# Where three feed-forward blocks split their gates into high and low halves: a change in the order around the first group of seven products

## The chip, the cores and the metric

The kernel runs on one core of one Trainium2 chip. The metric is the device time of one execution in microseconds (us); lower is better. The core has a matrix engine (PE, with its weight loads listed apart as PEld), a vector engine (DVE), a scalar engine (ACT), a general engine (POOL), and a queue (SP) from which nearly all DMA transfers are issued. Each engine works through its own row of instructions strictly in the order of the program; a semaphore holds an instruction until what it needs is there.

## The reference

Two layers of a streaming encoder on 256 positions of width 1024, all in float32. Each layer is a feed-forward block, a mixer (a convolution module in layer 0, latent attention in layer 1) and a second feed-forward block. There are thus four feed-forward blocks, and the change touches the second, third and fourth.

```python
def swiglu_ffn(h, w1, w3, w2):
    return (jax.nn.silu(h @ w1) * (h @ w3)) @ w2
...
for i in range(DEPTH):
    h = h + FFN_RES_WEIGHT * swiglu_ffn(rmsnorm(h, ffn_norm1[i]), ffn1_w1[i], ffn1_w3[i], ffn1_w2[i])
    m = rmsnorm(h, mix_norm[i])
    ...
    h = h + FFN_RES_WEIGHT * swiglu_ffn(rmsnorm(h, ffn_norm2[i]), ffn2_w1[i], ffn2_w3[i], ffn2_w2[i])
return rmsnorm(h, final_norm)
```

D_MODEL is 1024, D_FF is 2816.

## The kernel before

**Products in three parts.** Matrix products run on operands split into a high half (rounded) and a low half (the rest). `mm3` makes one product of three matrix instructions: row halves high times weight low (L332 in the profile, shown as `lo,X..`), high times high (L335) and row low times weight high (L336).

**Weight blocks.** A weight block is 128 x 2048 float32 (1 MB). SP fetches it to one of four `raw` buffers. ACT writes its high half `hi` in two casts of 128x1024, and DVE writes its low half `lo = raw - hi` in two subtractions of 128x1024 (ordinary blocks: L246 and L247; blocks of a group of seven: L214 and L200). `hi` and `lo` have five buffers each.

**Chunks.** A feed-forward block goes through its 2816 hidden columns in six chunks, `c` = 0 to 5. An ordinary chunk uses four weight blocks, two of `w1` and two of `w3`. After a chunk, for each of the two row blocks (`tb`), ACT applies silu (L956), DVE multiplies the two branches (L958, or L258 where it is marked urgent) and transposes 32x32 squares (L478), and five DMAs turn the gate through DRAM memory (L482 and L487). Then ACT casts the turned gate to its high half `Gh` and DVE writes its low half `Gl` (both L853). These casts and low splits are kept in the list `gates`, two pairs for each chunk; nothing on PE needs them before the down product `@ w2`, which starts after chunk 5.

**The group of seven.** In the second, third and fourth block, chunk 3 is a 2x2 product of submatrices done with seven products instead of eight (`seven_products`). Its weights are made by `load_seven`: four fetched blocks and four differences on DVE (128x2048, L200 `raw<-raw,raw`). The third of these differences, in `load_seven` at `j == 2`, is the one that makes the weight of the third product. PE adds the products into four banks c11, c21, c12 and c22, and three sums connect them: ACT copies c11 to c21 after the first product and c22 to `kept` after the second (both L258), DVE adds c21 and `kept` into c12 after the third product and into c22 after the fifth (both L258, `u<-u,p`). The order of the products is: c11, c22, c21, c11, c21, c12, c21. The same function also serves the first products of `@ w2`; there `late` is given and the lines of the change do nothing.

**What sets the order.** The program is written with a scheduler that orders each engine's row by its own timeline; `urgent` gives an operation priority, and `order(a, b)` adds the rule that a stands behind b on its engine. The change is in such rules.

Of the kernel before, what the change touches and what calls it, by code (L numbers as in the profile page):

```python
# [22 lines left out]
NT = S // P  # L23
# [19 lines left out]
PIECES = 2  # L43
# [46 lines left out]
def trunk(ctx: ExitStack, tc: tile.TileContext, x, xt, first, pos, invf, gfin, wdw,  # L90
          f1w13, f1w2, f2w13, f2w2, cw1, cw2, wa, wuq, wukv, wo, wpair, out):
    nc = tc.nc
# [12 lines left out]
    def uid(s):  # L105
        n_uid[0] += 1
        return f"{s}_{n_uid[0]}"
# [46 lines left out]
    def order(ins, first):  # L154
        tc.add_manual_dep(ins.ins, first.name, mybir.DependencyInfo(
            mybir.DependencyClass.NoSync, mybir.DependencyReason.DATA), reason="order")

    def behind(ins):

        for first in ahead_of.get(ins.ins.engine, [])[-BEHIND:]:  # L160
            order(ins, first)


    casts = {}

    turns = []
    last_read = [None]
# [14 lines left out]
    def fetched(src):  # L182
        raw = rawp.tile([P, HB], F32, tag="raw", name=uid("raw"))
        dma = nc.sync.dma_start(raw, src)
        if turns:
            order(dma, turns[-1].ins)
        return raw

    def load_seven(j, four, b, pieces):
        hi = wp.tile([P, HB], F32R, tag="hi", name=uid("hi"))  # L190
        lo = wp.tile([P, HB], F32R, tag="lo", name=uid("lo"))
        n = len(loaded)
        if j == 0:
            b[11], b[12] = fetched(four[0]), fetched(four[1])
        elif j == 1:
            b[22] = fetched(four[3])
        elif j == 2:
            b[21] = fetched(four[2])
        def sub(out, left, right):
            ins = nc.vector.tensor_sub(out, left, right)  # L200
            behind(ins)
            return ins

        if j == 1:
            sub(b[11], b[12], b[11])
            sub(b[12], b[22], b[12])
        elif j == 2:
            sub(b[11], b[22], b[11])
        elif j == 6:
            sub(b[11], b[21], b[11])  # L210
        raw = b[(11, 11, 11, 21, 12, 22, 11)[j]]
        for i in range(pieces):
            c = slice(i * HB // pieces, (i + 1) * HB // pieces)
            casts[n, i] = nc.scalar.copy(hi[:, c], raw[:, c]), sub(lo[:, c], raw[:, c], hi[:, c].bitcast(F32))  # L214
            behind(casts[n, i][0])
        return hi, lo

    def load(src, pieces=1):
        if isinstance(src, tuple) and src[0] == "seven":
            return load_seven(*src[1:], pieces)  # L220
# [31 lines left out]
    def urgent(f):  # L252

        def g(*args, **kw):
            traced = nc.cur_bb.bb.instructions
            n = len(traced)
            with tc.high_priority():
                r = f(*args, **kw)  # L258
            last = {ins.engine: ins for ins in traced[n:]}
            for engine, ins in last.items():  # L260
                ahead_of.setdefault(engine, []).append(ins)
            return r
        return g

    def load_ahead(ahead=W_BUFS - 2):
        load_to(min(len(blocks), n_used[0] + ahead))
# [5 lines left out]
    def weights(n=1, more=True):  # L272
        out = []
        for _ in range(n):
            n_used[0] += 1
            if more:
                load_ahead()
            else:
                load_ahead(0)
            out.append(loaded[n_used[0] - 1])  # L280
        return out
# [48 lines left out]
    def mm3(o, ah, al, bh, bl, start, stop, after=(), seeded=False):  # L330

        mm = nc.tensor.matmul(o, ah, bl, start=start, stop=False, skip_group_check=seeded)  # L332
        for a in after:
            order(mm, a.ins)
        nc.tensor.matmul(o, ah, bh, start=False, stop=False, skip_group_check=seeded)  # L335
        return nc.tensor.matmul(o, al, bh, start=False, stop=stop, skip_group_check=seeded)  # L336
# [31 lines left out]
    def seven_products(xh, xl, forms, banks, late={}):  # L368


        def rows(a, tb):
            k = slice(4 * a, 4 * a + 4)
            return xh[:, k, tbs(tb)], xl[:, k, tbs(tb)]

        def product(a, b, fresh):
            load_ahead(W_BUFS - 1)
            (hi, lo), = weights(1, False)
            for k in range(4):
                c = slice(k * 512, k * 512 + 512)
                before[:] = [mm3(b, a[0][:, k], a[1][:, k], hi[:, c], lo[:, c], fresh and k == 0, k == 3, before, True)]  # L380

        n0 = n_used[0]
        before = []
        c11, c21, c12, c22 = banks[0, 0], banks[1, 0], banks[0, 1], banks[1, 1]
        product(rows(0, 0), c11, True)
        first = urgent(nc.scalar.copy)(c21, c11)
        for cast in late.values():
            order(cast, first.ins)
        product(forms[0], c22, True)
        kept = tmp.tile([P, 512], F32, tag="s", name=uid("p5"))  # L390
        last = urgent(nc.scalar.copy)(kept, c22)
        product(forms[1], c21, False)
        add = urgent(nc.vector.tensor_add)(c12, c21, kept)
        order(casts[n0 + 5, 0][1], add.ins)
        for high, low in gates[-NT:] if not late else ():
            order(high, last.ins)
            order(low, add.ins)
        low_gates = [low for high, low in gates[-NT:] if not late]
        product(rows(1, 0), c11, False)
        product(forms[2], c21, False)  # L400
        add = urgent(nc.vector.tensor_add)(c22, c21, kept)
        order(casts[n0 + 6, 0][1], add.ins)
        for low in low_gates[1:]:
            order(low, casts[n0 + 6, PIECES - 1][1].ins)
        product(forms[3], c12, False)
        product(rows(1, 1), c21, False)
# [8 lines left out]
    def tbs(tb):  # L415
        return slice(tb * P, (tb + 1) * P)
# [336 lines left out]
    class Rows:  # L753
# [6 lines left out]
        def seven(self, forms, late):  # L760
            seven_products(self.zh, self.zl, forms, self.o, late)
# [72 lines left out]
    gates = []  # L834
# [7 lines left out]
    def ffn_in(act, X, make_next, beside, apart, seven_up, seven_down):  # L842
# [41 lines left out]
        for c in range(6):  # L884
# [9 lines left out]
            if c in seven_up:  # L894
                for key in ((0, 0), (0, 1), (1, 1), (1, 0)):
                    u[key] = bank("A", "u")
                seven_products(X.xh, X.xl, forms, {(tb, m): b for (m, tb), b in u.items()})
                beside()
                beside()
# [788 lines left out]
    class Rows512:  # L1688

        n = {"ht": 0, "hb": 0}  # L1690
# [109 lines left out]
def build(shapes):  # L1800
    import concourse.bacc as _bacc

    nc = _bacc.Bacc("TRN2", target_bir_lowering=False, num_devices=1, dynamic_dma_scratch_size=1024)
    args = [nc.dram_tensor(f"in_{n}", s, mybir.dt.from_np(np.dtype(d)), kind="ExternalInput").ap()
            for n, s, d in shapes]
    out = nc.dram_tensor("out", (S, D), F32, kind="ExternalOutput").ap()
    with tile.TileContext(nc, schedule_with_timeline_sim=True) as tc:
        trunk(tc, *args, out)
    return nc
# [9 lines left out]
```

## Time and profile before

| what | value |
|---|---|
| time before, median of 3 runs | 897.49 us (896.9 to 898.99) |
| the profiled execution's own time | 896.07 us |
| its span, first to last instruction | 894.3 us |
| PE busy | 886.9 us (99%) |
| DVE busy | 743.1 us (83%) |
| ACT busy | 571.8 us (64%) |
| mean granted clock of PE | 0.999 |

Rows of the timeline start with the time from the span's start and the busy time, both in us; then come engine, line of the kernel before, operation, what is written from what, shapes, and how many instructions are put together (x2). In brackets stands how long the engine sat idle just before, and what ended that. Buffer numbers are left out there.

### The profile page before, as it was taken

The numbers are of one execution on the slowest core, as the hardware profiler recorded it, in microseconds if no ns is written. First come the engines' busy times: TensorE is split into PE (matmuls) and PEld (weight loads), VectorE is DVE, ScalarE is ACT, GpSimd is POOL, SyncE is SP. The second block draws the span as 40 slices with busy tenths as digits, with TensorE's granted clock in tenths as the row PEclk, the third lists the DMA queues.
The fourth block names the chain that finished last, engine by engine and source line by source line (L and its number), as shares of the span: only waits on it lengthen the run. The fifth ranks groups of instructions, "written<-read, shape, count | busy, mean of one in ns | idle before, by whom it ended". The sixth has DMA issues, their size and how long they took to land.

```text
span 894.3 us, 12241 instructions
## 1 busy us (share of the span) xinstructions
PE 886.9 (99%) x4221; PEld 745.9 (83%) x4221; DVE 743.1 (83%) x1083; ACT 571.8 (64%) x993; POOL 104.2 (12%) x227
## 2 busy tenths in 40 slices
PE   9999999999999999999999999999999999999997
PEld 7888888898988888888888888888899888888886
DVE  6787789579998999999588989995768579989973
ACT  7966458488886646667375566673677566474752
POOL 1000000069962000000010000001400010000000
PEclk9999999999999999999999999999999999999999
DMA  9987629834215864939759369495635349378541
GB/s 330 375 303 274 232 59 355 295 121 172 106 60 194 289 258 144 374 109 388 259 175 339 118 218 357 123 392 182 223 142 189 141 154 342 104 260 317 180 196 48
DMA packets 71055, 198.94 MB, mean 222 GB/s; under 512 B 12369, under 2 KB 41937, under 8 KB 51665
## 3 DMA queue, kind: packets, MB, share of 16 engines
q1 hardware_dynamic: 70560, 197.47, 61.8%
q8 instruction: 33, 0.54, 0.2%
q10 hardware_dynamic: 432, 0.69, 0.2%
q14 instruction: 30, 0.24, 0.1%
HBM read 181.87 MB, written 16.25 MB: 222 GB/s over the span
## 4 chain that ended last, share of the span: by engine, by line
PE 92%; DVE 4%; ACT 2%; DMA 1%; issue 0%; SPq 0%; POOL 0%; DVEq 0%; ACTq 0%
PE u L336 16%; PE u L335 16%; PE u L332 16%; PE o L335 9%; PE o L336 9%; PE o L332 9%; PE gate L1005 2%; PE u L411 2%; DVE acc L1094 2%; PE u L1005 2%; PE tp L446 1%; PE a L335 1%; PE a L332 1%; PE a L336 1%; PE nope L336 1%; PE nope L332 1%
## 5 line engine op out<-in xcount | busy, mean ns | idle before, releaser
L247 DVE TENSOR_TENSOR lo<-raw,hi 128x1024 fp32r<-128x1024 f32 (+1 forms) x236 | 276.2, 1212 | 38.8 <-ACT hi L246 37.6
L246 ACT CAST hi<-raw 128x1024 fp32r<-128x1024 f32 (+1 forms) x238 | 236.8, 1044 | 89.3 <-DMA raw<-in_f2w 30.8
L332 PE MATMUL u<-lo,Xh 128*128 128x512 f32 x612 | 238.4, 389 | 0.1
L336 PE MATMUL u<-hi,Xl 128*128 128x512 f32 x612 | 238.3, 389 | 0.0
L335 PE MATMUL u<-hi,Xh 128*128 128x512 f32 x612 | 238.1, 389 | 0.0
L332 PEld LDWEIGHTS u<-lo,Xh 128*128 128x128 f32 x612 | 114.9, 188 | 24.5 <-ACT Xh L598 0.5
L336 PEld LDWEIGHTS u<-hi,Xl 128*128 128x128 f32 x612 | 114.9, 188 | 24.3 <-DVE Xl L465 0.5
L335 PEld LDWEIGHTS u<-hi,Xh 128*128 128x128 f32 x612 | 114.9, 188 | 23.8
L214 ACT CAST hi<-raw 128x1024 fp32r<-128x1024 f32 x98 | 97.7, 1050 | 51.8 <-DVE raw L200 44.9
L200 DVE TENSOR_TENSOR lo<-raw,hi 128x1024 fp32r<-128x1024 f32 x98 | 115.6, 1216 | 7.1 <-ACT hi L214 7.1
L332 PE MATMUL o<-lo,Gh 128*128 128x512 f32 (+1 forms) x276 | 106.6, 386 | 0.0
L335 PE MATMUL o<-hi,Gh 128*128 128x512 f32 (+1 forms) x276 | 106.5, 386 | 0.0
L336 PE MATMUL o<-hi,Gl 128*128 128x512 f32 (+1 forms) x276 | 106.5, 386 | 0.0
L437 POOL TENSOR_TENSOR ms<-ss 128x1 f32<-128x1 f32 x16 | 8.1, 510 | 597.6 <-ACT junk L429 597.6
L200 DVE TENSOR_TENSOR raw<-raw,raw 128x2048 f32<-128x2048 f32 x28 | 63.9, 2283 | 1.8 <-DMA raw<-in_f2w 0.9
L332 PEld LDWEIGHTS o<-lo,Gh 128*128 128x128 f32 x276 | 51.8, 188 | 10.5
L335 PEld LDWEIGHTS o<-hi,Gh 128*128 128x128 f32 x276 | 51.9, 188 | 10.5
L336 PEld LDWEIGHTS o<-hi,Gl 128*128 128x128 f32 x276 | 51.8, 188 | 10.4
L1094 DVE SCALAR_TENSOR_TENSOR acc<-V,dw,acc 128x128 f32<-128x128 f32 (+1 forms) x174 | 53.9, 391 | 0.0
L1115 ACT ACTIVATE prod<-V,dw 128x128 f32<-128x128 f32 (+1 forms) x128 | 45.6, 415 | 1.8 <-POOL Y L1116 1.0
L956 ACT ACTIVATE s<-u,R 128x512 f32<-128x512 f32 (+1 forms) x48 | 30.9, 647 | 24.8 <-PE u L336 24.1
L797 DVE SCALAR_TENSOR_TENSOR h<-o,rh,h 128x512 f32<-128x512 f32 (+1 forms) x18 | 12.9, 719 | 29.2 <-PE o L336 29.2
(265 smaller groups left out, 1257.7 us busy)
## 6 DMA issues: line engine op xcount, KB each, us to landing
raw<-in_f2w SPq DMA_DIRECT2D x66, 1024.0 KB, 6.2
raw<-in_f1w SPq DMA_DIRECT2D x62, 1024.0 KB, 6.5
raw<-in_cw SPq DMA_DIRECT2D x12, 1024.0 KB, 5.5
gd<-gt SPq DMA_DIRECT2D x160, 64.0 KB, 3.0
gb<-gd SPq DMA_DIRECT2D x24, 256.0 KB, 2.8
rows<-gd SPq DMA_DIRECT2D x16, 256.0 KB, 4.4
raw<-in_wo SPq DMA_DIRECT2D x4, 1024.0 KB, 4.9
hd<-rows SPq DMA_DIRECT2D x56, 64.0 KB, 2.4
```

Source lines behind the costliest of these rows:

```text
L200: ins = nc.vector.tensor_sub(out, left, right)
L214: casts[n, i] = nc.scalar.copy(hi[:, c], raw[:, c]), sub(lo[:, c], raw[:, c], hi[:, c].bitcast(F32))
L246: casts[len(loaded), i] = (nc.scalar.copy(hi[:, c], raw[:, c]), low.tensor_sub(lo[:, c], raw[:, c], hi[:, c].bitcast(F32)))
L247: low.tensor_sub(lo[:, c], raw[:, c], hi[:, c].bitcast(F32)))
L332: mm = nc.tensor.matmul(o, ah, bl, start=start, stop=False, skip_group_check=seeded)
L335: nc.tensor.matmul(o, ah, bh, start=False, stop=False, skip_group_check=seeded)
L336: return nc.tensor.matmul(o, al, bh, start=False, stop=stop, skip_group_check=seeded)
L411: mm = nc.tensor.matmul(o, al if kind == "x" else ah, bl if kind == "l" else bh, start=start and n == 0, stop=stop and n == len(kinds) - 1)
L956: nc.scalar.activation(s[:, :w], u[0, tb][:, :w], AF.Silu, scale=X.r[tb])
L1005: mm = nc.tensor.matmul(u[:, t], w[:, c], X.x[:, k, t], start=(k == 0), stop=(k == KT - 1))
L1094: dve_last.append(nc.vector.scalar_tensor_tensor(out if j == j1 - 1 else y, v, w, y, op0=ALU.mult, op1=ALU.add))
L1115: prods_last.append(nc.scalar.activation(p, v, AF.Copy, scale=w))
```

## The change

Two rules are replaced. For the third chunk's gates (`gates[-NT:]`, chunk 2): before, both casts stood behind the copy of c22 and both low splits behind the sum into c12, the second low split also behind the low half of the seventh block; now the first cast stands behind the sixth block's last high cast, the second behind the seventh block's last high cast, and both low splits behind the seventh block's last low half. For the second chunk's gates (`gates[-2 * NT:-NT]`, chunk 1): a new rule puts their low splits behind the third weight difference, which `load_seven` now keeps in `thirds`.

```diff
+    thirds = {}
...
         elif j == 2:
-            sub(b[11], b[22], b[11])
+            thirds[n] = sub(b[11], b[22], b[11])
...
         kept = tmp.tile([P, 512], F32, tag="s", name=uid("p5"))
-        last = urgent(nc.scalar.copy)(kept, c22)
+        urgent(nc.scalar.copy)(kept, c22)
         product(forms[1], c21, False)
         add = urgent(nc.vector.tensor_add)(c12, c21, kept)
         order(casts[n0 + 5, 0][1], add.ins)
-        for high, low in gates[-NT:] if not late else ():
-            order(high, last.ins)
-            order(low, add.ins)
-        low_gates = [low for high, low in gates[-NT:] if not late]
+        for high, low in gates[-2 * NT:-NT] if not late else ():
+            order(low, thirds[n0 + 2].ins)
+        late_gates = gates[-NT:] if not late else ()
         product(rows(1, 0), c11, False)
         product(forms[2], c21, False)
         add = urgent(nc.vector.tensor_add)(c22, c21, kept)
         order(casts[n0 + 6, 0][1], add.ins)
-        for low in low_gates[1:]:
+        for n, (high, low) in enumerate(late_gates):
+            order(high, casts[n0 + 5 + n, PIECES - 1][0].ins)
             order(low, casts[n0 + 6, PIECES - 1][1].ins)
```

PE's row is the same before and after. Below are pieces of the rows of DVE and ACT in the second feed-forward block, the first of the three; the other two blocks change in the same way. All lines of the changed kernel that stand behind the new line have a number higher by one.

On DVE around the end of the group of seven, before. `lo_3434`, `lo_3453` and `lo_3473` are the low halves of the sixth block, the seventh block and the next chunk's first block; `u_3393` is c12, `u_3392` is c22, `u_3391` is c21; `Gl_2854` is the gates' low half, from the turned gates `gb_3372` and `gb_3386` of the third chunk; `s_3532` is the group's own gate of the first row block; `raw_3235<-raw_3305,raw_3235` is the fourth weight difference:

```order
L258 TENSOR_TENSOR u_3393<-u_3391,p_553_3431 128x512
L853 TENSOR_TENSOR Gl_2854<-gb_3372,Gh_2853 128x4x128
L200 TENSOR_TENSOR lo_3434<-raw_3295,hi_3433 128x1024
L200 TENSOR_TENSOR raw_3235<-raw_3305,raw_3235 128x2048
L200 TENSOR_TENSOR lo_3434<-raw_3295,hi_3433 128x1024
L258 TENSOR_TENSOR u_3392<-u_3391,p_553_3431 128x512
L200 TENSOR_TENSOR lo_3453<-raw_3235,hi_3452 128x1024 x2
L853 TENSOR_TENSOR Gl_2854<-gb_3386,Gh_2853 128x4x128
L247 TENSOR_TENSOR lo_3473<-raw_3471,hi_3472 128x1024
L258 TENSOR_TENSOR s_3532<-s_3532,u_3393 128x512
L247 TENSOR_TENSOR lo_3473<-raw_3471,hi_3472 128x1024
```

The same place in the row of DVE after:

```order
L201 TENSOR_TENSOR lo_3434<-raw_3295,hi_3433 128x1024
L259 TENSOR_TENSOR u_3393<-u_3391,p_553_3431 128x512
L201 TENSOR_TENSOR lo_3434<-raw_3295,hi_3433 128x1024
L201 TENSOR_TENSOR raw_3235<-raw_3305,raw_3235 128x2048
L259 TENSOR_TENSOR u_3392<-u_3391,p_553_3431 128x512
L201 TENSOR_TENSOR lo_3453<-raw_3235,hi_3452 128x1024 x2
L854 TENSOR_TENSOR Gl_2854<-gb_3372,Gh_2853 128x4x128
L854 TENSOR_TENSOR Gl_2854<-gb_3386,Gh_2853 128x4x128
L259 TENSOR_TENSOR s_3532<-s_3532,u_3393 128x512
L248 TENSOR_TENSOR lo_3473<-raw_3471,hi_3472 128x1024 x2
```

The sixth block's low half moves ahead, to both sides of the first sum; both low splits of the third chunk's gates now stand behind the seventh block's low half, and with the multiplication of the gate `s_3532` they stand ahead of `lo_3473`.

On ACT at the same place, before. `hi_3433`, `hi_3452` and `hi_3472` are the high halves of the same three blocks, `Gh_2853` is the gates' high half, and `p_553_3431` is `kept`:

```order
L258 COPY p_553_3431<-u_3392 128x512
L853 CAST Gh_2853<-gb_3372 128x4x128
L214 CAST hi_3433<-raw_3295 128x1024 x2
L956 ACTIVATE s_3532<-u_3390,R_2792 128x512
L853 CAST Gh_2853<-gb_3386 128x4x128
L214 CAST hi_3452<-raw_3235 128x1024 x2
L246 CAST hi_3472<-raw_3471 128x1024 x2
```

And after:

```order
L259 COPY p_553_3431<-u_3392 128x512
L215 CAST hi_3433<-raw_3295 128x1024 x2
L854 CAST Gh_2853<-gb_3372 128x4x128
L957 ACTIVATE s_3532<-u_3390,R_2792 128x512
L215 CAST hi_3452<-raw_3235 128x1024 x2
L854 CAST Gh_2853<-gb_3386 128x4x128
L247 CAST hi_3472<-raw_3471 128x1024 x2
```

Each of the two gate casts has moved behind the weight cast that it stood ahead of.

On DVE some 20 us earlier, where the group's first weights are made, before. `lo_3294` and `lo_3304` belong to the second and third block, `raw_3235<-raw_3295,raw_3235` is the third weight difference, and `Gl_2854<-rows_139` are the low splits of earlier chunks' gates:

```order
L200 TENSOR_TENSOR lo_3294<-raw_3235,hi_3293 128x1024 x2
L853 TENSOR_TENSOR Gl_2854<-rows_139,Gh_2853 128x4x128 x2
L200 TENSOR_TENSOR raw_3235<-raw_3295,raw_3235 128x2048
L344 TENSOR_TENSOR rows_139<-rows_139 128x512 x2
L200 TENSOR_TENSOR lo_3304<-raw_3235,hi_3303 128x1024
```

And after:

```order
L201 TENSOR_TENSOR lo_3294<-raw_3235,hi_3293 128x1024 x2
L201 TENSOR_TENSOR raw_3235<-raw_3295,raw_3235 128x2048
L854 TENSOR_TENSOR Gl_2854<-rows_139,Gh_2853 128x4x128 x2
L201 TENSOR_TENSOR lo_3304<-raw_3235,hi_3303 128x1024
L345 TENSOR_TENSOR rows_139<-rows_139 128x512
```

The two low splits and the third weight difference have changed places. Further on, where the next chunks' weights are made, some operations change places by one to three rows on ACT, DVE and SP (the fourth chunk's gates a little earlier against the down product's weights).

## The prediction

> **What bounds the kernel now.** I read the page first, then the waits of PE, then the timeline of DVE, ACT and PE's weight loads around the end of one group of seven.
>
> ```profile
> span 894.3 us, 12241 instructions
> PE 886.9 (99%) x4221; PEld 745.9 (83%) x4221; DVE 743.1 (83%) x1083; ACT 571.8 (64%) x993; POOL 104.2 (12%) x227
> PEclk9999999999999999999999999999999999999999
> PE u L411 <- ACT Xh L640: 0.2, 1, 0.2
> ```
>
> PE is busy 99% of the span at full granted clock; the last row, of PE's waits, is a wait of 0.2 us at the very start. So PE sets the end, and this change leaves PE's row as it is: it can gain only what PE waits for now, which is nearly nothing, and it can lose whatever makes PE wait. The question is how early the weights' low halves are. The timeline of DVE at the end of the first group:
>
> ```profile
> 348.83 0.70 DVE L258 TENSOR_TENSOR u<-u,p 128x512 f32<-128x512 f32 x1 [1.53 <-PE u L336]
> 349.44 0.68 DVE L853 TENSOR_TENSOR Gl<-gb,Gh 128x512 fp32r<-128x512 f32 x1
> 350.03 1.22 DVE L200 TENSOR_TENSOR lo<-raw,hi 128x1024 fp32r<-128x1024 f32 x1
> 351.17 2.29 DVE L200 TENSOR_TENSOR raw<-raw,raw 128x2048 f32<-128x2048 f32 x1
> 353.37 1.22 DVE L200 TENSOR_TENSOR lo<-raw,hi 128x1024 fp32r<-128x1024 f32 x1
> 354.51 0.69 DVE L258 TENSOR_TENSOR u<-u,p 128x512 f32<-128x512 f32 x1
> 355.11 2.35 DVE L200 TENSOR_TENSOR lo<-raw,hi 128x1024 fp32r<-128x1024 f32 x2
> 357.38 0.69 DVE L853 TENSOR_TENSOR Gl<-gb,Gh 128x512 fp32r<-128x512 f32 x1
> 357.98 1.22 DVE L247 TENSOR_TENSOR lo<-raw,hi 128x1024 fp32r<-128x1024 f32 x1
> 359.12 0.68 DVE L258 TENSOR_TENSOR s<-s,u 128x512 f32<-128x512 f32 x1
> ```
>
> From 348.83 on DVE has no hole. The row at 357.98 is the first half of `lo_3473`, the low half of the next chunk's first block; it ends at 357.98 + 1.22 = 359.20. PE's weight loads and matmuls there:
>
> ```profile
> 348.33 0.39 PE L336 MATMUL u<-hi,Gl 128*128 128x512 f32 x1
> 353.77 0.39 PE L336 MATMUL u<-hi,Gl 128*128 128x512 f32 x1
> 358.76 0.19 PEld L335 LDWEIGHTS u<-hi,Xh 128*128 128x128 f32 x1
> 358.99 0.19 PEld L336 LDWEIGHTS u<-hi,Xl 128*128 128x128 f32 x1
> 359.25 0.19 PEld L332 LDWEIGHTS u<-lo,Xh 128*128 128x128 f32 x1
> ```
>
> The first two are the last matmuls of the third and fifth products: 24 matmuls, two products, lie between them in 5.44 us, so the pace is 0.227 us. The load at 359.25 is the first that needs `lo_3473`. It comes 0.26 behind the one before, not 0.23: it starts 0.05 after that low half ends, so PE meets it with no reserve. The other two groups show the same picture, DVE first, then PE's load:
>
> ```profile
> 532.14 1.22 DVE L247 TENSOR_TENSOR lo<-raw,hi 128x1024 fp32r<-128x1024 f32 x1
> 533.42 0.19 PEld L332 LDWEIGHTS u<-lo,Xh 128*128 128x128 f32 x1
> 796.70 1.22 DVE L247 TENSOR_TENSOR lo<-raw,hi 128x1024 fp32r<-128x1024 f32 x1
> 797.97 0.19 PEld L332 LDWEIGHTS u<-lo,Xh 128*128 128x128 f32 x1
> ```
>
> Ends at 533.36 and 797.92, loads 0.06 and 0.05 later.
>
> **The change, part one: DVE at the end of the group.** Nothing is added or removed; rows change places. I follow the new row from the point that PE ties. The first sum starts at 348.83, 0.50 after the third product's last matmul starts (348.33), and DVE had waited 1.53 us for it. The second sum needs the fifth product, so it cannot start before 353.77 + 0.50 = 354.27. Before, it started at 354.51, because DVE was not free earlier; in the new row the first half of the sixth block's low half moves into the 1.53 us hole and a gate split (0.60) moves away, so DVE is free. How early: the second half of the sixth block then follows the first sum at 348.83 + 0.60 = 349.43, takes 1.14 from start to start (353.37 to 354.51), and the fourth difference takes 2.20 (351.17 to 353.37): free at 352.77. So DVE now stands idle for 1.5 us and the second sum starts at 354.27, 0.24 earlier than before. That is all that the freed time brings.
>
> Behind it the new row has, start to start: the second sum 0.60 (354.51 to 355.11), the seventh block's low half 2.27 (355.11 to 357.38), two gate splits at 0.60 (357.38 to 357.98), the gate's multiplication 0.59 (359.12 to its successor, which the trace has at 359.71, 0.09 before the 0.68 are over). `lo_3473` starts at 354.27 + 0.60 + 2.27 + 1.20 + 0.59 = 358.93, and its first half ends at 360.15, against 359.20 before: 0.95 later. Put shortly: one more split (0.60) and the multiplication (0.59) are in front of it, and 0.24 is won at the sum. The gate's multiplication waits for nothing new: its c12 is complete after the sixth product, 353.77 + 0.23 + 12 x 0.227 = 356.7, well before its turn.
>
> Nothing covers this: the load at 359.25 had 0.05 us. What a late load costs on PE is seen in one place of the trace, at the start of the second feed-forward block:
>
> ```profile
> 285.12 0.19 PEld L336 LDWEIGHTS u<-hi,Xl 128*128 128x128 f32 x1
> 285.84 0.19 PEld L332 LDWEIGHTS u<-lo,Xh 128*128 128x128 f32 x1 [0.54 <-ACT Xh L598]
> 285.34 0.39 PE L336 MATMUL u<-hi,Xl 128*128 128x512 f32 x1
> 286.41 0.39 PE L336 MATMUL u<-hi,Xl 128*128 128x512 f32 x1
> ```
>
> The load at 285.84 is 0.49 behind its time (285.12 + 0.23 = 285.35), and three matmuls on, 286.41 stands where 285.34 + 3 x 0.227 = 286.02 was due: 0.39 lost for 0.49 of lateness, 0.10 absorbed. Here the load comes at 360.15 + 0.05 = 360.20 where 358.99 + 0.23 = 359.22 was due: 0.98 late, 0.88 lost, of which 0.03 was lost before too. So 0.85 us for each group. The granted clock is not in this: the page has 9 in every slice, the slice of 285 us too.
>
> A bound from above: nothing absorbed and each of the eight steps 0.02 longer, 1.1 us a group. From below: the second sum starts as the fifth product's last matmul ends, at 354.16, and the four small steps take 0.03 less each, since the shortest multiplication of this kind is 649 ns where the one here took 0.68:
>
> ```profile
> L258 DVE TENSOR_TENSOR s<-s,u x12: 649/678/686, 339.4 to 802.5; 128x512 f32<-128x512 f32 x12
> ```
>
> That is 0.11 + 0.12 = 0.23 less, 0.62 a group. I take 0.85, which uses the durations of this very place.
>
> One rule of the Trainium skill speaks for more. The row: the pair at 355.11 takes 2.35 together, not 2 x 1.22 = 2.44, and its successor starts at 357.38 while the pair ends at 357.46. The Trainium skill, page "VectorE: DVE Perf Modes", section "The DRAIN you can't avoid", says that the next operation does not start until the pipeline has emptied. By that rule seven steps would each end before the next starts, seven times some 0.08, and the loss would be about 1.4 us a group; the row shows the overlap, so the measurement decides and this sum keeps it.
>
> **Part two: ACT at the same place.** Each gate cast moves behind a weight cast:
>
> ```profile
> 346.85 0.62 ACT L853 CAST Gh<-gb 128x512 fp32r<-128x512 f32 x1 [0.23 <-DMA gb<-gd]
> 347.38 1.99 ACT L214 CAST hi<-raw 128x1024 fp32r<-128x1024 f32 x2
> 352.78 0.62 ACT L853 CAST Gh<-gb 128x512 fp32r<-128x512 f32 x1 [0.62 <-DMA gb<-gd]
> 353.49 2.00 ACT L214 CAST hi<-raw 128x1024 fp32r<-128x1024 f32 x2
> 355.39 2.00 ACT L246 CAST hi<-raw 128x1024 fp32r<-128x1024 f32 x2
> ```
>
> The sixth block's cast (347.38) starts up to 0.53 earlier, ahead of the gate cast at 346.85, which lets its low half into the hole. The seventh block's cast now follows the fourth difference at 352.9 and ends at 354.8; the second gate cast (0.62) runs behind it, and `hi_3472` starts again at about 355.4. DVE asks for that cast's first half at 358.93: 2.5 us of cover. Cost nothing.
>
> **Part three: the second chunk's low splits behind the third difference.**
>
> ```profile
> 330.57 1.34 DVE L853 TENSOR_TENSOR Gl<-rows,Gh 128x512 fp32r<-128x512 f32 x2 [0.55 <-ACT Gh L853]
> 331.82 2.29 DVE L200 TENSOR_TENSOR raw<-raw,raw 128x2048 f32<-128x2048 f32 x1
> 335.36 1.22 DVE L200 TENSOR_TENSOR lo<-raw,hi 128x1024 fp32r<-128x1024 f32 x1
> 338.83 0.68 DVE L344 TENSOR_TENSOR rows<-rows 128x512 f32<-128x512 f32 x1
> ```
>
> The difference takes the place of the 0.55 wait, so the third block's low half is ready a little earlier than its 336.6. PE needs it 12 matmuls ahead of the fourth product, whose first stands 0.23 behind the row at 348.33: 348.56 - 2.72 = 345.8. Both orders have 9 us of cover: cost and gain nothing. Two sums of rows (L344, the last row) slide in between the third chunk's gate multiplications and transposes, so its turn through memory starts up to 1.4 us later (2 x 0.68); the rival below prices that.
>
> **Part four: the fourth chunk's gates and SP.** Their turned gates are fetched ahead of the down product's first weights on SP, and their low split stands ahead of these weights' low half.
>
> ```profile
> 375.17 2.36 DVE L200 TENSOR_TENSOR lo<-raw,hi 128x1024 fp32r<-128x1024 f32 x2 [0.75 <-ACT hi L214]
> 378.83 0.62 ACT L853 CAST Gh<-gb 128x512 fp32r<-128x512 f32 x1 [2.74 <-DMA gb<-gd]
> ```
>
> These weights are ready at 377.5, and PE reaches them after six ordinary blocks of 24 matmuls, at 359.4 + 32.6 = 392. A split of 0.6, or a wait of the 2.74 us in the last row, is hidden: cost nothing. In the down product's own group a first low half moves ahead of a difference and the second stays behind both, so the block is complete at the same time.
>
> **The sum.** 3 groups x 0.85 = 2.6 us. PE has no later wait into which this could vanish. The profiled execution's own time is 896.07 (span 894.3 and 1.8 around it); made against it the sum gives 898.7. That execution lies 1.4 below the median of the runs, 897.49, and against the median the sum gives 900.1, 0.29% slower. About 0.2% of the time, 1.8 us, is what a measurement of this kernel tells from no change.
>
> **The rivals.**
>
> *The late load is mostly made up* (0.12). All of the lower bounds hold at once: 0.62 a group, 1.9 in all, 899.4, on the edge of 0.2%; half of this chance counts as the same. For it: the new row gives ACT and DVE more lead ahead of the second sum. Against it: that lead ends at the sum, which PE ties.
>
> *DVE passes the waiting sum* (0.04). Were DVE to run ready work past an instruction that waits, the two splits would fill the new 1.5 us hole from 352.77, and `lo_3473` would start at 354.27 + 0.60 + 2.27 + 0.59 = 357.73 and end at 358.95, 0.25 before now. Then PE gains its 0.03 a group and the time is 897.4: not slower. It decides from about 0.95 us of passed work a group. Against it: in the hole before 348.83 a gate split whose cast ended at 347.47 (346.85 + 0.62) stood behind the waiting sum and did not run.
>
> *The turned gate lands late* (0.05). The second gate cast now stands ahead of `hi_3472` on ACT. If its data came after 357.2, the first half of `hi_3472` (0.62 + 1.05 later) would be later than 358.93, and each us more costs a us a group: landing at 358.2 gives 3 x 1.85, 903.0. It was there at 352.78; 1.4 later by part three is 354.2, which leaves 3 us.
>
> *Every DVE step ends before the next starts* (0.02), worked out from the rows' full durations: 0.95 + 7 x 0.08 = 1.5 late, 1.4 lost a group, 901.7. It is the rule of the Trainium skill weighed above; the trace of before speaks against it.
>
> **How the numbers follow.** The forecast has the remaining 0.77. Its own bounds are 0.62 to 1.1 a group, 899.4 to 900.8; the runs of before spread from 0.6 below to 1.5 above their median. The range is 898.6 to 901.9: it holds most of the first rival and the fourth, and leaves out the second and third. Slower by over 0.2% (above 899.3): 0.77 and both dear rivals, half of the first rival, less some 0.05 for a median that falls low, 0.85. Faster has no mechanism: 0.02. The rest, 0.13, is the same.
>
> **What would show it.** In the profile after: PE's first load for `lo_3473` and its two counterparts about 1 us behind the load before it, with DVE named as the releaser, three times, and no other new wait of PE; the second sum at 0.50 after the fifth product's last matmul begins, behind an idle stretch of DVE of about 1.5 us; ACT never the last. It is wrong if those loads follow the one before within 0.3 us, if the lateness differs by over 0.3 us from 0.98, or if PE waits anew in the down product's group.

## Result and the profile after

The changed kernel takes 898.87 us (median of 21 runs, 897.67 to 900.16) where the kernel before takes 896.97 in the same runs (21): a ratio of 1.0020, 95% interval 1.0014 to 1.0026, so 1.9 us slower. 900.1 was forecast. The profiled execution took 899.55 us; its span is 897.8 us and its mean granted clock 0.998 (0.999 before). The waits of PE's weight loads after, the two longest in total and one further down:

```profile
PEld u L333 <- DVE lo L248: 3.0, 3, 1.0
PEld u L333 <- ACT Xh L599: 1.5, 3, 0.8
PEld o L333 <- DVE lo L201: 0.4, 1, 0.4
```

The first row is new: three waits of 1.0 us for a low half of an ordinary block, one in each of the three groups. The second row, at the starts of feed-forward blocks, differs from execution to execution, before as after. The third is one load of the down product's own group of seven in the fourth feed-forward block; more on it below. The timeline of DVE at the end of the first group, after (all lines are one higher):

```profile
349.01 1.22 DVE L201 TENSOR_TENSOR lo<-raw,hi 128x1024 fp32r<-128x1024 f32 x1 [1.25 <-ACT hi L215]
350.15 0.69 DVE L259 TENSOR_TENSOR u<-u,p 128x512 f32<-128x512 f32 x1
350.75 1.21 DVE L201 TENSOR_TENSOR lo<-raw,hi 128x1024 fp32r<-128x1024 f32 x1
351.88 2.29 DVE L201 TENSOR_TENSOR raw<-raw,raw 128x2048 f32<-128x2048 f32 x1
354.65 0.70 DVE L259 TENSOR_TENSOR u<-u,p 128x512 f32<-128x512 f32 x1 [0.48 <-PE u L337]
355.29 2.36 DVE L201 TENSOR_TENSOR lo<-raw,hi 128x1024 fp32r<-128x1024 f32 x2
357.57 1.29 DVE L854 TENSOR_TENSOR Gl<-gb,Gh 128x512 fp32r<-128x512 f32 x2
358.77 0.68 DVE L259 TENSOR_TENSOR s<-s,u 128x512 f32<-128x512 f32 x1
359.37 2.35 DVE L248 TENSOR_TENSOR lo<-raw,hi 128x1024 fp32r<-128x1024 f32 x2
```

And PE's weight loads there:

```profile
359.44 0.19 PEld L337 LDWEIGHTS u<-hi,Xl 128*128 128x128 f32 x1
360.64 0.19 PEld L333 LDWEIGHTS u<-lo,Xh 128*128 128x128 f32 x1 [1.01 <-DVE lo L248]
361.21 0.19 PEld L333 LDWEIGHTS u<-lo,Xh 128*128 128x128 f32 x1
```

Behind the second sum stand the seventh block's low half, both splits, the multiplication, and only then `lo_3473` at 359.37. PE's load comes 1.20 us behind the load before it, against 0.26 before. In the other two groups it is 1.20 as well (loads at 535.81 and 801.21). Four loads behind the one at 359.44, the load at 361.21 was due at 359.44 + 4 x 0.227 = 360.35: PE has lost 0.86 us here, and the same in the other two groups.

The third wait above is this row, 0.60 us behind the load before it, so some 0.37 late:

```profile
850.46 0.19 PEld L333 LDWEIGHTS o<-lo,Gh 128*128 128x128 f32 x1 [0.42 <-DVE lo L201]
```

### The profile page after: what moved, and what is told of

Same layout as the page of the kernel before. It is cut to its first block, busy times and chain, and to the rows that moved or that the text cites. A ratio compares the mean times of both kernels' runs of the same rounds, so it can differ in the third digit from the quotient of the medians.

```text
span 897.8 us, 12256 instructions
## 1 busy us (share of the span) xinstructions
PE 888.4 (99%) x4221; PEld 745.8 (83%) x4221; DVE 744.5 (83%) x1083; ACT 571.1 (64%) x993; POOL 104.1 (12%) x227
## 4 chain that ended last, share of the span: by engine, by line
PE 93%; DVE 3%; DMA 2%; ACT 1%; SPq 0%; issue 0%; ACTq 0%; DVEq 0%
PE u L333 16%; PE u L337 16%; PE u L336 16%; PE o L333 9%; PE o L337 9%; PE o L336 9%; PE u L1006 3%; PE gate L1006 3%; PE u L412 2%; DMA hd<-rows 1%; PE tp L447 1%; PE pairs L1049 1%; PE a L337 1%; PE a L336 1%; PE a L333 1%; PE nope L333 1%
```

## Experiments

The theory is that of the forecast: what stands ahead of `lo_3473` on DVE makes PE wait, by its own length. The first rival is that the second chunk's part costs the time. A question came with the result: the trace shows 3 x 0.86 = 2.6 us lost at the three places, and the times only 1.9.

**The third chunk's rules alone.**

```diff
-        for high, low in gates[-2 * NT:-NT] if not late else ():
-            order(low, thirds[n0 + 2].ins)
```

> Only the third chunk's rules are changed; the second chunk's low splits stay where they were before. Theory (two gate splits and the multiplication stand ahead of the next chunk's first low half): DVE's row at the end of the group is that of the changed kernel, so PE's three loads come 1.2 us behind the load before them and the time is that of the changed kernel, about 1.9 us above before. Rival (the loss comes from the second chunk's splits behind the third difference): loads 0.26 behind, time as before.

899.11 us against 897.56: ratio 1.0016 (1.0006 to 1.0025). The wait is the changed kernel's:

```profile
PEld u L333 <- DVE lo L248: 3.0, 3, 1.0
```

PE's three loads come 1.19, 1.20 and 1.19 behind the one before. The loss is in the third chunk's rules.

**The second chunk's rule alone**, on the kernel before.

```diff
+            thirds[n] = sub(b[11], b[22], b[11])
...
+        for high, low in gates[-2 * NT:-NT] if not late else ():
+            order(low, thirds[n0 + 2].ins)
```

> Only the second chunk's low splits are put behind the third weight difference; the third chunk keeps the rules of before. Theory: 9 us of cover, so the three loads stay 0.26 behind the load before them and the time is within 0.3 us of before. Rival (the loss comes from this part): about 1.9 us slower than before.

897.36 us, ratio 0.9993 (0.9982 to 1.0005); the three loads come 0.26, 0.26 and 0.34 behind the one before. No loss shows, and the interval excludes one of 1.9 us. The first rival falls.

**Both splits behind the next chunk's low half**, an edit of the changed kernel.

```diff
             order(high, casts[n0 + 5 + n, PIECES - 1][0].ins)
-            order(low, casts[n0 + 6, PIECES - 1][1].ins)
+            order(low, casts[n0 + 7, PIECES - 1][1].ins)
```

> The changed kernel, but both of the third chunk's low splits stand behind the next chunk's first low half instead of ahead of it. Theory: 1.2 us of DVE's row leave the way, that low half is ready about 0.25 before PE asks for it, the three loads come 0.23 behind the load before them, 2.6 us less than the changed kernel by the trace. If executions of the kernel before lose some 0.2 us a group at this place that its profiled execution does not show, this kernel is 0.6 faster than before; if not, it is at before's time. Rival (the wait is not set by these two splits): time of the changed kernel.

896.49 us, ratio to before 0.9988 (0.9980 to 0.9997). This beats both kernels. DVE's timeline in the first group:

```profile
356.55 2.36 DVE L201 TENSOR_TENSOR lo<-raw,hi 128x1024 fp32r<-128x1024 f32 x2
358.82 0.68 DVE L259 TENSOR_TENSOR s<-s,u 128x512 f32<-128x512 f32 x1
359.42 1.22 DVE L248 TENSOR_TENSOR lo<-raw,hi 128x1024 fp32r<-128x1024 f32 x1
360.56 0.70 DVE L479 STREAM_TRANSPOSE gt<-s 128x512 f32<-128x512 f32 x1
361.18 1.19 DVE L248 TENSOR_TENSOR lo<-raw,hi 128x1024 fp32r<-128x1024 f32 x1
362.29 1.28 DVE L854 TENSOR_TENSOR Gl<-gb,Gh 128x512 fp32r<-128x512 f32 x2
```

Only the multiplication is left ahead of `lo_3473`, both splits follow at 362.29, and no load of the three is more than 0.25 behind the one before. So the two splits' place is the loss. Against the changed kernel, which has the same order on ACT, the ratios (1.0020 and 0.9988) are 2.9 us apart with some 0.9 either way, where the trace of the changed kernel has 2.6. That the kernel is 1.1 us below before, and not just at it, speaks for a loss in the kernel before that its profiled execution doesn't show.

**One split less, one split more.** Two doses: the first split ahead of the second sum, where the changed kernel's DVE is idle; and a third split, the second one written twice, ahead of `lo_3473`.

```diff
-            order(low, casts[n0 + 6, PIECES - 1][1].ins)
+            order(low, casts[n0 + 6, PIECES - 1][1].ins if n else casts[n0 + 5, PIECES - 1][1].ins)
+            if n == 0:
+                order(add, low.ins)
```

> The changed kernel, but the first of the two low splits stands ahead of the second sum, where the changed kernel's DVE is idle for 0.48 us. Theory: the split takes 0.60, so the second sum starts 0.12 later and the next chunk's first low half 0.48 earlier than in the changed kernel; PE's loads come about 0.72 behind the load before them instead of 1.20, some 0.48 a group or 1.4 us less than the changed kernel. Rival (a late load costs PE a fixed amount, not by its size): no gain against the changed kernel.

```diff
+            if c + 1 in seven_up and tb == 1:
+                again[:] = [nc.vector.tensor_sub(low, bv, gh.bitcast(F32))]
...
+        for low in again if not late else ():
+            order(low, casts[n0 + 6, PIECES - 1][1].ins)
+            for i in range(PIECES):
+                order(casts[n0 + 7, i][1], low.ins)
```

> The changed kernel with a third split ahead of the next chunk's first low half: the second low split of the third chunk's gates is written twice with the same values. Theory (each operation ahead of that low half costs PE its own length): 0.60 more a group, PE's three loads 1.80 behind the load before them, 1.8 us more than the changed kernel, some 3.7 above before. Rival (the lateness is taken up elsewhere, since already the changed kernel costs less in its times than in its trace): less than 1 us more than the changed kernel.

With one split less: 897.38 us, ratio 0.9993 (0.9984 to 1.0002), 2.4 us below the changed kernel by the ratios where 1.4 was expected. With one more: 900.65 us, 1.0034 (1.0022 to 1.0046), 1.3 us above the changed kernel where 1.8 was expected. Both differences are uncertain by about 1 us, so the second time alone does not exclude its rival, less than 1 us more; the loads decide between them. Waits of the loads, one split less, then one more:

```profile
PEld u L333 <- DVE lo L248: 1.4, 4, 0.4
```

```profile
PEld u L334 <- DVE lo L249: 4.8, 3, 1.6
```

The loads come 0.60, 0.59, 0.59 behind the one before in the first kernel, 1.80, 1.79, 1.80 in the second, and 1.20 in the changed one: each split of 0.60 us counts in full. (The fourth wait of the first kernel, 0.2 us, lies in the first 30 us of the run.) I had expected 0.72 for the first kernel, since I read the idle stretch as 0.48. In the changed kernel the second sum starts 0.57 after DVE could have started it (351.88 + 2.20 = 354.08, against 354.65), so the split fits almost whole.

**The kernel before, profiled twice more**, and with one edit: its second split behind `lo_3473`.

> The kernel before, profiled a second time. If its executions differ at the three places, the loads for the next chunk's first low half come more than 0.3 us behind the load before them in one or more groups here; if they don't, all three are at 0.26 again, and what differs from execution to execution lies elsewhere.

> The kernel before, profiled a third time: as for the second profile, three loads at 0.26 or some of them above 0.3.

```diff
         for low in low_gates[1:]:
-            order(low, casts[n0 + 6, PIECES - 1][1].ins)
+            order(low, casts[n0 + 7, PIECES - 1][1].ins)
```

> The kernel before with one edit: the second low split of the third chunk's gates stands behind the next chunk's first low half. That gives this low half 0.60 us of reserve, which the kernel before lacks. If other executions of the kernel before lose time there that its profiled execution doesn't show, this kernel is 0.6 to 1.1 us faster than before, like the one with both splits behind; if they don't, it is at most 0.1 faster, and the gain of that one comes from the rest of the change.

The two profiles (898.37 and 897.87 us) show a wait that the first profile of before does not have. The load for the **seventh block's** low half, one block earlier than expected, comes 1.31 behind the load before it in the third group of one, and 0.65 and 0.91 in the first and third group of the other; each time the load for `lo_3473` or its counterpart follows 0.44 to 0.47 behind the one before it. PE's loads, and ACT and DVE ahead of them, in the second profile's third group:

```profile
797.05 0.19 PEld L332 LDWEIGHTS u<-lo,Xh 128*128 128x128 f32 x1 [1.12 <-DVE lo L200]
799.93 0.19 PEld L332 LDWEIGHTS u<-lo,Xh 128*128 128x128 f32 x1 [0.28 <-DVE lo L247]
```

```profile
793.60 0.62 ACT L853 CAST Gh<-gb 128x512 fp32r<-128x512 f32 x1 [3.41 <-DMA gb<-gd]
794.12 0.69 ACT L956 ACTIVATE s<-u,R 128x512 f32<-128x512 f32 x1
794.70 1.99 ACT L214 CAST hi<-raw 128x1024 fp32r<-128x1024 f32 x2
793.99 0.69 DVE L258 TENSOR_TENSOR u<-u,p 128x512 f32<-128x512 f32 x1
795.77 2.36 DVE L200 TENSOR_TENSOR lo<-raw,hi 128x1024 fp32r<-128x1024 f32 x2 [1.10 <-ACT hi L214]
```

The gate cast stands ahead of the seventh block's cast on ACT and waits 3.41 us for its turned gate; in the same group of the first profile it was this row:

```profile
789.38 0.62 ACT L853 CAST Gh<-gb 128x512 fp32r<-128x512 f32 x1 [1.25 <-DMA gb<-gd]
```

On SP the fetch of that gate waited for the writes of the turned gate (`gd`), and was issued at 790.86 where the first profile has 786.72; the waits of SP from 775 to 800 us and its timeline in the second profile:

```profile
SPq L487 <- DMA gd<-gt: 4.9, 2, 3.6
790.86 0.34 SPq L487 DMA_DIRECT2D gb<-gd  x1
```

So the kernel before does lose time that its profile did not show, but at another place and from another cause than I had asked for. Each late group loses about a load's lateness less 0.1: in the second profile 1.31 - 0.23 - 0.10 and 0.47 - 0.23 - 0.10, 1.1 us; in the third 0.3 + 0.6 and two of 0.1, 1.1 us; in the first none. That is about half of what the two executions lie above the first one (896.07); the rest is at other places. The kernel with the one edit took 896.86 us, ratio 0.9995 (0.9986 to 1.0004), not clear of no change: its loads for `lo_3473` are in time, but in its third group the seventh block's load is still 0.99 behind the one before:

```profile
796.11 0.19 PEld L332 LDWEIGHTS u<-lo,Xh 128*128 128x128 f32 x1 [0.80 <-DVE lo L200]
```

By the trace, then, the reserve at `lo_3473` does not remove this loss; the times alone do not settle it, since their interval reaches down to 1.3 us below before.

**ACT's part alone**, shown against the kernel before. Casts as in the changed kernel, and on DVE the order before `lo_3473` as before: one split ahead, the multiplication held behind its first half. The second chunk's rule is left out.

```diff
-            order(high, last.ins)
             order(low, add.ins)
...
+            order(high, casts[n0 + 5 + n, PIECES - 1][0].ins)
+            if n:
+                order(low, casts[n0 + 6, PIECES - 1][1].ins)
...
+                if c in seven_up and tb == 0:
+                    order(times, casts[n_used[0], 0][1].ins)
```

> Of the change only ACT's part: the gate casts stand behind the weight casts as in the changed kernel; on DVE the second low split stays ahead of the next chunk's first low half, as before, and a rule of its own holds the group's gate multiplication behind the first half of that low half, also as before. Theory (the casts' part removes a wait for the turned gates' DMA that the kernel before has in part of its executions, while DVE's part costs 2.6 us): no gate cast waits ahead of the seventh block's cast, the seventh product's load and the three loads behind it come within 0.3 us of the load before them, and the time is 0.6 to 1.1 us below before. Rival (the casts' part gives nothing, and the gain of the kernel with both splits behind comes from DVE alone): time of the kernel before, within 0.3.

> The kernel with both low splits behind the next chunk's first low half, a second time, beside the one with the casts' part alone: 0.6 to 1.1 us below before, no load of the three above 0.3 us behind the load before it, no wait for a gate cast ahead of a weight cast on ACT. If its first result was chance, it is at before's time.

896.31 us with the casts' part alone, ratio 0.9990 (0.9979 to 1.0000); 896.12 us for the kernel with both splits behind, again, 0.9986 (0.9976 to 0.9995). Before took 897.26 beside them. ACT's timeline in the third group, casts' part alone:

```profile
785.67 2.00 ACT L214 CAST hi<-raw 128x1024 fp32r<-128x1024 f32 x2
787.56 0.62 ACT L854 CAST Gh<-gb 128x512 fp32r<-128x512 f32 x1
790.62 0.69 ACT L957 ACTIVATE s<-u,R 128x512 f32<-128x512 f32 x1 [2.44 <-PE u L336]
792.89 2.00 ACT L214 CAST hi<-raw 128x1024 fp32r<-128x1024 f32 x2 [1.58 <-DVE raw L200]
794.80 0.61 ACT L854 CAST Gh<-gb 128x512 fp32r<-128x512 f32 x1
```

No gate cast waits here, and no load of a seventh block or of `lo_3473`'s kind is late. Over all profiles: with the casts moved, 7 profiles and 21 groups, none has a late seventh block; with the casts as before, 5 profiles and 15 groups, four have. In two of the seven at least, this is not because the gate came early. In the three late third groups (second and third profile of before, and its one edit), SP issued the second gate's fetch 5.1, 5.5 and 5.4 us before the seventh block's load was due. With the third chunk's rules alone it did so 5.0 us ahead (793.05, load at 798.02), and in the second measurement with both splits behind 5.4 (790.26, load at 795.62), and neither load is late. With the third chunk's rules alone even the first gate's cast waited 2.23 us there, and the next weight cast, at 795.27, still had to wait 1.58 us for its weight difference:

```profile
792.27 0.62 ACT L852 CAST Gh<-gb 128x512 fp32r<-128x512 f32 x1 [2.23 <-DMA gb<-gd]
793.05 0.34 SPq L486 DMA_DIRECT2D gb<-gd  x1
798.02 0.19 PEld L333 LDWEIGHTS u<-lo,Xh 128*128 128x128 f32 x1
```

The gain in the times, about 0.1%, has an interval that reaches 1.0000 for the casts alone; the two measurements of the kernel with both splits behind stay clear of it.

## Why the prediction was right, point by point

- *PE sets the end, and only a late low half matters*: right. The new waits at the three places are those of the low half, and PE loses 2.6 us by them.
- *The second sum is tied to PE, the lead in front of it is lost*: right. It waits for PE after as well (354.65, idle 0.48). The size of the idle stretch was wrong, 1.5 us forecast. The step that failed is that the sixth block's low half fills the earlier hole: it stood still in it for 1.25 us, until 349.01, and both of its casts were done at 348.98. In the built program of the changed kernel the half ahead of the first sum is the second one (columns 1024 to 2047), whose cast is last; the rule that binds the low half to the sum, `order(casts[n0 + 5, 0][1], add.ins)`, names the first half only. So the first sum came 0.86 later than PE allowed (350.15 against 348.79 + 0.50), and that much of the lead was gone. No term of the sum hung on it, since the second sum still waited for PE.
- *`lo_3473` 0.95 later, its load 0.98 behind its time*: 360.64 against 359.44 + 0.23 = 359.67, 0.97. All steps of the row are there, starts overlapping ends by some 0.08 as in the trace of before. Small differences nearly cancel: the second sum starts 0.42 after the fifth product's last matmul begins (354.23), not 0.50, and takes 0.64 to its successor, not 0.60. The rival by full durations did not come. The section of the Trainium skill that it was taken from ("VectorE: DVE Perf Modes", "The DRAIN you can't avoid") goes on to say that an operation that is not held starts earlier; the prediction left that out, and the rows go with it.
- *2.6 us in all*: this term was mis-sized against the times. The loss in the trace is as forecast, 0.86 a group, and the times show 1.9. The step that failed is "it can gain only what PE waits for now, which is nearly nothing", and with it "Cost nothing" under "ACT at the same place". Both were read from one execution in which the turned gates came early. In two other executions the kernel before lost 1.1 us each by a gate cast that held up a weight cast. The change takes that exposure away. The kernels with the casts moved and no late low half are 0.9 to 1.3 us below before, and within their intervals that is what lies between 2.6 and 1.9. The mean over the three profiles of before is 0.7 us as well, but three executions are too few to call that a measurement.
- *900.1, and a range of 898.6 to 901.9*: the measured 898.87 lies in the range, but below the forecast's own bounds of 899.4 to 900.8. About 0.5 of the 1.2 us between 900.1 and 898.87 is the starting point (897.49 from three runs, 896.97 from 21), and 0.7 the difference just described. What keeps the time in the range is the width given to it for the spread of the runs, not a term of the sum; to that extent it was luck. "Slower by over 0.2%" came out on its edge, 0.20%.
- *Second chunk and later moves cost nothing*: right for the second chunk within the interval of that run. For the down product's group the profile after has what was named as a sign of being wrong: one load there is 0.37 late (850.46). It is not shown that the change does this. The kernel before has a load 0.16 late at the same place in its second profile (849.30), and the kernels with the third chunk's rules alone, one split less and one split more have the changed order of DVE there and no late load.
- *The rivals*: the lateness was not made up; the 1.9 us of the first rival is the measured number, but not by its mechanism, since each group loses 0.86 in the trace and not 0.62. DVE passed no waiting sum: the first split's cast was done at 349.49, and DVE stood idle ahead of the sum at 354.65 all the same. No gate cast waited ahead of `hi_3472`. A late gate was priced only for the kernel after; where it cost time was the kernel before, one weight cast earlier.

## What to carry to other kernels

Where an engine's row feeds the bound engine without reserve, as DVE's row did here, each operation put ahead of the due one costs its full length; count what stands between the last point that the bound engine ties and the operation that it waits for. Work that nobody waits for belongs behind the due operation on every engine, not only on the one that was looked at: here the casts' move on ACT gained and the splits' move on DVE lost, and with the splits one block further back the kernel beats both. A wait for a DMA can be short in one profile and long in the next, so ask of an instruction ahead of a due one not how long it waited, but what it waits for.

## What was not expected of the hardware

The turn of a gate through memory varies much between executions of one program: the second gate cast of the same group waited 1.25, 3.41 and 2.38 us for its data in three profiles of the kernel before (the third at 793.53). In its first group it was 0.62, 0.78 and 1.86 us. Part of such a wait is only that ACT came free earlier. SP's row shows the memory's part: from the end of the issue of the gate's four writes to the issue of the fetch that waits for them it was 1.7 us (784.98 to 786.72), 3.8 (787.02 to 790.86) and 2.9 (787.91 to 790.77) in the third group of the three profiles.
